# The product with w_out of a hybrid encoder block, as seven products of sums of quarters

## The chip, the cores and the metric

One Trainium2 chip, one of its cores. The program is one launch that computes the whole block. Five engines run side by side, each with its own instruction stream: TensorE (PE, matmuls and transposes), VectorE (DVE), ScalarE (ACT), GpSimd (POOL) and SyncE (SP, which here only issues transfers). Transfers move between DRAM and the on-chip memory (SBUF) on 16 DMA engines. Matmuls write into banks of PSUM, from which DVE or ACT read them ("evict"). The metric is the device time of one launch in microseconds (us).

## The reference

x is 1024 tokens by 1024 features, float32; 16 meta tokens are put ahead and dropped at the end.

```python
u = rmsnorm(h, norm_mix)
a, q, k, v, r, lr, ga, gb = split(u @ w_in)
p = multiscale_pool(a) through w_pool_mix, times pool_scale
y_a = p @ w_pool_out
log_a = log_sigmoid(lr @ w_gate_up + b_gate) / 16
o = gla_chunked(q * 64 ** -0.5, k, v, log_a)        # chunks of 64 tokens
o = rmsnorm(o, gla_norm) * silu(r)
y_b = o @ w_gla_out
m = sigmoid(ga) * y_a + sigmoid(gb) * y_b
h = h + m @ w_out                                    # 1024 x 1024 by 1024 x 1024
h = h + square(relu(rmsnorm(h, norm_ffn) @ w_ff1)) @ w_ff2
out = rmsnorm(h, norm_final)
```

The change is about the line `h + m @ w_out` and what stands beside it.

## The kernel before

Every product runs on PE in a float32 of two parts: an operand a is split into `hi` (rounded by an ACT copy) and `lo = a - hi` (a DVE subtract), and `mm3` (L275 and on) issues three matmuls per block of 128 of the contraction: hi x hi, hi x lo, lo x hi. So each weight or token that enters a product costs one ACT copy and one DVE subtract of its size.

The stages, in order of time: norm and transposes of x; the projections with w_in (with weights and tokens added and subtracted in quarters, so that four products become fewer); pooling; decays; the chunked attention, in two halves of 512 tokens (half 0 first), between whose steps blocks of `y_a` and `y_b` are poured; the merge stage; the first and second feed-forward layer (FF1, FF2), each by seven products of sums of quarters.

The merge stage, where the change lies, spans about 447 to 588 us:

- `yb_block(j, h)`: columns 256 j to 256 j + 255 of y_b for half h, two tiles of 128 columns (e = 0, 1), four k each. DVE evicts with the gate (L1195), adds y_a's part (L1196), ACT makes the hi (L1199) and DVE the lo (L1200) of m, in `MH[h]`, `ML[h]`. The gates and y_a's parts come back from DRAM (`gb_dram`, `ma_dram`) on SP's queue, by `ask` and `take`. Weights of w_gla_out come through the ring `W1` (two slots) and its raw buffers: load on SP, ACT copy at L84, DVE subtract at L85, tile names `raw`, `w1h`, `w1l`.
- `load_wo(ch, kk)`: a quarter of a column half of w_out, loaded on SP, split at L1344 (ACT) and L1345 (DVE) into `wo`.
- `out_tile(t, ch)`: the product for 128 tokens and 512 columns: eight k, 24 matmuls into a bank `mm` of which there are three; DVE adds it at L1379 onto `acc`, into which `x_again` had loaded x on SP. Behind the second column half comes `layer_norm` (ACT square L251, two small ACT operations, three small ones on DVE, the scaled row L259) and a store to `h_dram`.
- `turn_tile(t)`: eight PE transposes of a normed tile into banks `ms`, with ACT copies and splits for FF1, woven in two tiles behind the product.

PE's order is the order in which the code is written (`manual_schedule`); on the other engines the scheduler of the Tile layer puts instructions in an order at build time, by priorities that follow the order of the code, and each engine then runs its list strictly in order. A waiting instruction holds up all behind it on its engine. In the kernel before, POOL has 58 rows: sums of w_in's weights (L810) and a few others; all transfers of the stage are issued by SP.

Of the kernel before, what the change touches and what calls it, by code (L numbers as in the profile page):

```python
# [96 lines left out]
class Raw:  # L97
# [11 lines left out]
    def load(self, ap, n):  # L109
        while any(self.slots[self.n % len(self.slots)] is t for t in self.held):  # L110
            self.n += 1
        self.last = self.slots[self.n % len(self.slots)]
        dst = self.last[:, :n]
        self.n += 1
        view = dst
        if len(ap.shape) == 3:
            view = dst.rearrange("p (a b) -> p a b", a=ap.shape[1])
        self.nc.sync.dma_start(view, ap)
        return dst
# [3 lines left out]
def kernel(  # L123
# [55 lines left out]
    h_dram = dp.tile([8, P, D], F32, name="h_dram")  # L179
    hf_dram = [dp.tile([NPAIR, P, HALF], F32, name=f"hf{m}_dram") for m in range(7)]  # L180
# [425 lines left out]
    def decays(p):  # L606
        def fn():
# [6 lines left out]
            if p:  # L614
                act.activation(gnorm, gnorm, ACT.Copy, scale=0.5)
# [75 lines left out]

    def differences():
# [394 lines left out]
    def gla_open():  # L1087
        left.pop_to(S["left_t"])
        right.pop_to(0)
        S["yg"] = {h: right.push(f"yg{h}", [P, 2, HEADS, HALF], F32R) for h in (1, 0)}  # L1090
# [9 lines left out]
        wanted[:] = [("a", d, h) for d in range(8) for h in range(2)] + [("b", d, 0) for d in range(8)]  # L1100
# [68 lines left out]
    KEPT = (2, 3)  # L1169
    kept = {}  # L1170

    def yb_block(j, h):
        def fn(wb=None):
# [7 lines left out]
            yg = S["yg"][h]  # L1181
            for e in range(2):
                d, w = 2 * j + e, slice(e * P, (e + 1) * P)
                ask()
                gl, ml = take("b", d, h)
# [11 lines left out]
                th = MH[h][:, d]  # L1197
                tl = ML[h][:, d]
                act.activation(th, gl, ACT.Copy, scale=0.5)  # L1199
                dve.scalar_tensor_tensor(tl, gl, 0.5, f32(th), ALU.mult, ALU.subtract)  # L1200
# [132 lines left out]

    def load_wo(ch, kk):
        def fn():
            wo = S["wo"][ch][:, :, 2 * kk : 2 * kk + 2]
            c = slice(ch * HALF, (ch + 1) * HALF)
            src = w_out[kk * 256 : (kk + 1) * 256, c].rearrange("(k p) c -> p k c", p=P)
            if ch:
                r = raw.load(src, D).rearrange("p (k c) -> p k c", k=2)  # L1340
            else:
                r = S["acc"][:, 4 + kk].rearrange("p (k c) -> p k c", k=2)
                nc.sync.dma_start(r, src)
            act.activation(wo[:, 0], r, ACT.Copy)  # L1344
# [4 lines left out]
    step(rest, merge_open)
    def wo1_open():  # L1350
        raw.back()
        left.pop_to(S["left2"])
        right.pop_to(0)
        S["u2p"] = right.push("u2p", [P, 2, HALF], F32)
        raw.lend(right.push("rawx0", [P, D], F32))
        S["right_ff"] = right.mark()
        S["wo"].append(right.push("wo1", [P, 2, KT, HALF], F32R))


    ORDER = (0, 4, 1, 5, 2, 3, 6, 7)  # L1360

    def out_tile(t, ch):
        def fn():
            half, at = t // 4, (t % 4) * P
            wo = S["wo"][ch]
            if ch == 0 and t < 6:
                x_again(t + 2)
            if ch == 0 and t == 6:
                act.activation(gB, gB, ACT.Copy, scale=-0.5)
            b, n = bank("mm"), ORDER.index(t)  # L1370
            for j in range(2):
                if ch and j and n > 1:
                    turn_tile(ORDER[n - 2])
                mm3(
                    b, KT // 2, lambda i: (MH[half][:, 4 * j + i, at : at + P], ML[half][:, 4 * j + i, at : at + P]),
                    lambda i: (wo[:, 0, 4 * j + i], wo[:, 1, 4 * j + i]), first=j == 0, last=j == 1,
                )
            a = S["acc"][:, t, ch * HALF : (ch + 1) * HALF]
            dve.tensor_tensor(a, b, a, ALU.add)  # L1379
            if ch:  # L1380
                layer_norm(S["acc"][:, t], S["u2"][:, n % 2])
                nc.sync.dma_start(h_dram[t], S["acc"][:, t])

        return fn

    def turn_tile(t, tags=("ms",)):
# [3 lines left out]
        u, acc, g = S["u2"][:, ORDER.index(t) % 2], S["acc"], t % 4  # L1390
# [348 lines left out]
```

## Time and profile before

| what | value |
|---|---|
| time, median of 3 runs | 1210.76 us (1210.07 to 1211.37) |
| profiled execution, span from first to last instruction | 1209.1 us (its own time on the device is not listed; the median lies 1.7 us above the span) |
| mean granted PE clock | 0.998 |
| PE / DVE / ACT / POOL busy | 99% / 69% / 48% / 7% |
| bytes moved by DMA | 192.79 MB, mean 159 GB/s |

Times are read from one profiled execution. "Busy" is the time in which an engine executes an instruction; PE's instructions overlap, so a matmul of 0.39 us follows the one before by less. A group row reads: line, engine, operation, output<-input by names, shape, xcount | busy us, mean ns of one | idle time before them and who ended it. A row of the timeline reads: start, duration, engine, line, operation, and in brackets the idle time before it.

### The profile page before, as it was taken

Reading aid. Unit: us, or ns where it says so; the run is one execution under the profiler, and the core shown is the slowest. Engines: PE = TensorE matmul, PEld = TensorE weight load, DVE = VectorE, ACT = ScalarE, POOL = GpSimd, SP = SyncE. Lnnn points to the kernel's source line nnn. Section 1 sums busy time; section 2 is a strip of 40 time slices with the busy share of each in tenths; the row PEclk is TensorE's granted clock in tenths of the full one; section 3 lists DMA queues with packets and bytes.
Section 4 is the critical chain, followed back from the end, with each engine's and each line's share of the span. In section 5 each row is a group of like instructions: output and inputs, shape, how many; then the busy total and the mean of one; then the engine's idle time right before and its main releaser. Section 6 shows DMA issues by size and latency. Waiting matters only on the chain.

```text
span 1209.1 us, 18303 instructions
## 1 busy us (share of the span) xinstructions
PE 1194.4 (99%) x6775; PEld 993.1 (82%) x6775; DVE 837.5 (69%) x1369; ACT 574.4 (48%) x1014; POOL 79.1 (7%) x97
## 2 busy tenths in 40 slices
PE   9999999999999999999999999999999999999997
PEld 7999877878778887788788888888888888888886
DVE  6636567565686669726887767677675887887686
ACT  7546444444456124305655545455464444444554
POOL 0000062323320000000000000000000000000000
PEclk9999999999999999999999999999999999999999
DMA  8223253534348978812255444444479963333532
GB/s 245 77 60 123 91 133 110 166 110 146 112 138 296 315 218 268 284 32 87 88 161 168 151 139 157 148 160 151 152 253 318 348 229 98 98 100 91 173 96 88
DMA packets 151385, 192.79 MB, mean 159 GB/s; under 512 B 12216, under 2 KB 86256, under 8 KB 151296
## 3 DMA queue, kind: packets, MB, share of 16 engines
q1 hardware_dynamic: 151136, 191.56, 49.5%
q8 instruction: 53, 0.87, 0.3%
q14 instruction: 36, 0.29, 0.1%
q10 hardware_dynamic: 160, 0.07, 0.0%
HBM read 128.66 MB, written 62.93 MB: 158 GB/s over the span
## 4 chain that ended last, share of the span: by engine, by line
PE 68%; DVE 3%; issue 1%; DMA 1%; ACT 1%; DVEq 0%; ACTq 0%
PE b_oa L287 5%; PE b_oa L285 5%; PE b_oa L286 5%; PE b_y L285 4%; PE b_y L286 4%; PE b_y L287 4%; PE b_mm L285 4%; PE b_mm L287 4%; PE b_mm L286 4%; PE b_ob L287 4%; PE b_ob L285 4%; PE b_ob L286 4%; PE b_z L286 3%; PE b_z L285 3%; PE b_z L287 3%; PE b_sc L285 2%
## 5 line engine op out<-in xcount | busy, mean ns | idle before, releaser
L774 ACT ACTIVATE w1h<-raw 128x512 fp32r<-128x512 f32 x106 | 65.8, 622 | 51.2 <-PE b_sc L286 21.2
L285 PE MATMUL b_sc<-th,w1h 128*128 128x512 f32 x216 | 85.4, 395 | 0.4 <-ACT u2p L1522 0.4
L285 PE MATMUL b_z<-th,w1h 128*128 128x512 f32 x216 | 84.9, 393 | 0.4 <-DVE c L893 0.4
L775 DVE TENSOR_TENSOR w1l<-raw,w1h 128x512 fp32r<-128x512 f32 x106 | 72.5, 685 | 18.0 <-ACT w1h L774 18.0
L286 PE MATMUL b_sc<-tl,w1h 128*128 128x512 f32 x216 | 84.8, 393 | 0.0
L286 PE MATMUL b_z<-tl,w1h 128*128 128x512 f32 x216 | 84.2, 390 | 0.4 <-DVE tl L1408 0.4
L287 PE MATMUL b_sc<-th,w1l 128*128 128x512 f32 x216 | 84.4, 391 | 0.0
L287 PE MATMUL b_z<-th,w1l 128*128 128x512 f32 x216 | 84.1, 389 | 0.0
L774 ACT ACTIVATE w1h<-fs 128x512 fp32r<-128x512 f32 x81 | 51.1, 630 | 67.0 <-PE b_y L286 33.6
L775 DVE TENSOR_TENSOR w1l<-fs,w1h 128x512 fp32r<-128x512 f32 x81 | 57.7, 712 | 23.7 <-ACT w1h L774 23.7
L285 PE MATMUL b_mm<-th,w1h 128*128 128x512 f32 (+1 forms) x208 | 72.0, 346 | 0.0
L287 PE MATMUL b_mm<-th,w1l 128*128 128x512 f32 (+1 forms) x208 | 71.1, 342 | 0.0
L286 PE MATMUL b_mm<-tl,w1h 128*128 128x512 f32 (+1 forms) x208 | 71.0, 342 | 0.0
L774 ACT ACTIVATE w1h<-bt 128x512 fp32r<-128x512 f32 x46 | 29.1, 632 | 70.8 <-issue 43.9
L1598 DVE TENSOR_TENSOR bt<-w,w 128x512 f32<-128x512 f32 x80 | 54.7, 683 | 2.7 <-DMA w<-in_w_ff_dram 2.7
L285 PE MATMUL b_mm<-wo,th 128*128 128x512 f32 x128 | 50.4, 394 | 0.9 <-PE b_mm L287 0.9
L287 PE MATMUL b_mm<-wo,tl 128*128 128x512 f32 x128 | 49.9, 390 | 0.0
L286 PE MATMUL b_mm<-wo,th 128*128 128x512 f32 x128 | 49.8, 389 | 0.0
L285 PE MATMUL b_y<-wo,w1h 128*128 128x512 f32 x128 | 49.8, 389 | 0.0
L286 PE MATMUL b_y<-wo,w1h 128*128 128x512 f32 x128 | 49.8, 389 | 0.0
L287 PE MATMUL b_y<-wo,w1l 128*128 128x512 f32 x128 | 49.8, 389 | 0.0
L775 DVE TENSOR_TENSOR w1l<-bt,w1h 128x512 fp32r<-128x512 f32 x46 | 31.8, 691 | 25.6 <-ACT w1h L774 25.6
(425 smaller groups left out, 3317.1 us busy)
## 6 DMA issues: line engine op xcount, KB each, us to landing
hf_dram<-h SPq DMA_DIRECT2D x112, 256.0 KB, 2.1
raw<-hf_dram SPq DMA_DIRECT2D x112, 256.0 KB, 2.6
w<-in_w_ff_dram SPq DMA_DIRECT2D x64, 256.0 KB, 4.8
raw<-in_w_in_dram SPq DMA_DIRECT2D x22, 512.0 KB, 4.7
raw<-in_w_ff_dram SPq DMA_DIRECT2D x16, 512.0 KB, 4.1
rawx<-in_w_ff_dram SPq DMA_DIRECT2D x16, 512.0 KB, 4.1
rawp<-in_w_in_dram SPq DMA_DIRECT2D x10, 512.0 KB, 4.2
xs<-in_x_dram SPq DMA_DIRECT2D x8, 512.0 KB, 4.8
```

The source lines that it names most:

```text
L285: pe.matmul(ps, ah, bh, start=first and i == 0, stop=False, skip_group_check=more)
L286: pe.matmul(ps, ah, bl, start=False, stop=False, skip_group_check=more)
L287: pe.matmul(ps, al, bh, start=False, stop=last and i == n - 1, skip_group_check=more)
L774: act.activation(hi, a, ACT.Copy)
L775: dve.tensor_tensor(lo, a, f32(hi), ALU.subtract)
L1598: dve.tensor_tensor(bt, w, S["w2"][q[3:]][:, i], ALU.add if q[2] == "+" else ALU.subtract)
```

## The change

m (tokens by features) and w_out are each taken as two by two quarters of 512 by 512, and the product is made of seven products P1 to P7 of 512 x 512 x 512, four token tiles and four k each, instead of eight.

- Four sums of w_out's quarters are made in DRAM at the program's start: for each, a copy and an accumulating transfer, on POOL's queue (`sums_of_w_out`). Two of them are built on each other: the fourth on the third, the third on the second.
- Sums of m's quarters are made where y_b is finished: `split_to` and subtracts on DVE, `in_two` (two 128x256 halves) on POOL. One quarter of half 0 is stored to `a21_dram` and loaded again by POOL.
- Weights (`bring`) and x (`x_quarter`: a direct load and an accumulating one for each column half) come on POOL's queue, as loads of 1 MB or 2 x 512 KB. The lo parts of some weights are made by POOL (`parts(p, pool)`).
- The banks are mm 2, x 2, ms 2 instead of mm 3, ms 3; P1's first two tiles use the two-bank tile `b_sc`.
- m is kept without the factor 0.5, which moves into other scales (gnorm 0.25, pscale 0.5). Half 1's tokens come first in `acc` and at the end (`tokens`). w_gla_out's columns are taken as j and j + 4, loaded by two transfers.

The core of the diff:

```diff
+    def sums_of_w_out():
+        u1, u2, u3, u4 = sums_dram
+        b11, b12, b21, b22 = (w_out_quarter(j) for j in range(4))
+        for to, first, second in ((u1, b11, b12), (u3, b22, b12), (u2, u3, b11), (u4, u2, b21)):
+            pool.dma_start(to, first)
+            pool.dma_start(to, second, accum_op=ALU.add)
+
+    def in_two(op, to, a, b):
+        for c in (slice(0, 256), slice(256, HALF)):
+            pool.tensor_tensor(to[:, c], a[:, c], b[:, c], op)
...
+    step(one, lambda: sums_of_w_out())
...
                 dve.scalar_tensor_tensor(gl, gl, 1.0, b, ALU.add, ALU.mult)
                 dve.tensor_tensor(gl, gl, ml, ALU.add)
-                th = MH[h][:, d]
-                tl = ML[h][:, d]
-                act.activation(th, gl, ACT.Copy, scale=0.5)
-                dve.scalar_tensor_tensor(tl, gl, 0.5, f32(th), ALU.mult, ALU.subtract)
+                m.append(gl)
+                if h:
+                    after_half1(j, e, gl)
+                elif e == 0:
+                    nc.sync.dma_start(a21_dram[j], gl)
+                else:
+                    split_to(quarter(1), j, gl)
+                    dve.tensor_tensor(gl, m[0], gl, ALU.subtract)
+                    split_to(quarter(2), j, gl)
...
+    def after_half1(k, e, m):
+        s2, s3 = S["acc"][:, 4 + k, :HALF], S["tmp"][:, k]
+        if e == 0:
+            split_to(quarter(3), k, m)
+            in_two(ALU.subtract, s3, m, s3)
+            dve.tensor_tensor(s2, s2, m, ALU.subtract)
+            split_to(far(1), k, s2)
+        else:
+            split_to(S["w"][1], k, m)
+            in_two(ALU.add, s2, m, s2)
...
-        banks(keep=2, ms=3)
+        banks(keep=1, mm=2, x=2, ms=2)
...
+    def parts(p, eng=dve):
+        hi, lo = weights_of(p)
+        for k, a in enumerate(landed.pop(p)):
+            act.activation(hi[:, k], a, ACT.Copy)
+            if eng is pool:
+                in_two(ALU.subtract, lo[:, k], a, f32(hi[:, k]))
             else:
+                dve.tensor_tensor(lo[:, k], a, f32(hi[:, k]), ALU.subtract)
...
+        mm3(b, 4, lambda k: (ah[:, k, c], al[:, k, c]), lambda k: (wh[:, k], wl[:, k]), first=first, more=not first)
+        if p == "P5":
+            act.activation(c22, b, ACT.Copy)
+            return
...
+    out_products("P5", 0, 1, 2, 3)
+    later(lambda: parts("P2"))
+    yb(0)
+    later(second_copy)
+    later(lambda: x_quarter(1, 1, True))
+    yb(1)
+    later(lambda: bring("P1", two_raws()))
+    later(lambda: x_quarter(0, 0))
+    later(lambda: x_quarter(0, 1, True))
+    later(third_parts)
+    later(lambda: bring("P6", [S["tmp"]]))
+    out_products("P2", 0)
+    later(lambda: parts("P1", pool))
+    out_products("P2", 1, 2, 3)
...
+    later(lambda: bring("P4", two_raws()))
+    later(lambda: parts("P7", pool))
+    later(lambda: parts("P4", pool))
+    later(early_blocks)
+    out_products("P6", 0, 1)
+    out_products("P3", 0)
+    out_products("P6", 2)
+    out_products("P3", 1)
+    out_products("P6", 3)
+    later(turn_tile, 0)
```

How the built order moves, at three places. First DVE where half 0's y_b is finished, before: from one split of w_gla_out's weights (L85) to the next; `sr` and `yg` belong to the attention's output, `o` and `c` are tiles of m.

```order
L85 TENSOR_TENSOR w1l<-raw_116,w1h 128x1024
L1269 TENSOR_TENSOR sr_3829<-b_m_4528,sr_3829 128x1024
L1196 TENSOR_TENSOR o<-o 128x512
L1195 SCALAR_TENSOR_TENSOR o<-o,b_mm 128x512
L1272 TENSOR_TENSOR yg_3805<-sr_3829,yg_3805 128x1024
L1200 SCALAR_TENSOR_TENSOR tl_136<-o,th_132 128x512
L1196 TENSOR_TENSOR o<-o,t_985 128x512
L1269 TENSOR_TENSOR sr_3833<-b_sc,sr_3833 128x1024
L1200 SCALAR_TENSOR_TENSOR tl_136<-o,th_132 128x512
L85 TENSOR_TENSOR w1l<-raw_120,w1h 128x1024
```

The same engine and place in the changed program, the last ten rows up to the second split (L1237 and L1238 are the evict and the add, L1210 the lo parts, L1246 the new subtract).

```order
L1238 TENSOR_TENSOR o<-o,t_990 128x512
L1237 SCALAR_TENSOR_TENSOR t_990<-t_990,b_mm 128x512
L1330 TENSOR_TENSOR fo<-sr_3843,fo 128x1024
L1210 TENSOR_TENSOR tl_141<-o,th_137 128x512
L1238 TENSOR_TENSOR t_990<-t_990 128x512
L1246 TENSOR_TENSOR o<-o 128x512
L1237 SCALAR_TENSOR_TENSOR c<-c,b_mm 128x512
L1210 TENSOR_TENSOR tl_149<-o,th_145 128x512
L1238 TENSOR_TENSOR c<-c 128x512
L85 TENSOR_TENSOR w1l<-raw_125,w1h 128x1024
```

Between the two splits stand 13 instructions now, ten of them 512 wide, where eight stood, five of them 512 wide.

Second POOL, in the changed program, behind half 1's last y_b block: L713 are its half operations, L1432 loads of weights, L1409 the direct load of an x quarter. In the program before, POOL has nothing at this place.

```order
L713 TENSOR_TENSOR tmp<-acc,tmp 128x256 x2
L713 TENSOR_TENSOR wo_4714<-raw_121,wo_4714 128x256 x2
L713 TENSOR_TENSOR wo_4714<-raw_125,wo_4714 128x256 x4
L1432 DMA raw_121<-in_w_out_dram 128x2x512
L713 TENSOR_TENSOR acc<-acc 128x256 x2
L1432 DMA raw_125<-in_w_out_dram 128x2x512
L1409 DMA acc<-in_x_dram 128x4x512
L1432 DMA tmp<-sum_dram 128x4x512
```

The load of x for the first column half, which SP issued before, stands behind eight half operations and two loads of weights.

Third ACT ahead of the first norm, before: splits of w_out (L1344) and of the first w_ff1 block (L774), then the square of the norm (L251).

```order
L1344 ACTIVATE wo_4933<-raw_120 128x1024
L774 ACTIVATE w1h<-raw_116 128x512 x2
L1344 ACTIVATE wo_4933<-rawx_4929 128x1024
L774 ACTIVATE w1h<-rawx_4929 128x512 x2
L251 ACTIVATE u_4679,small<-acc 128x1024
```

In the changed program (L1439 are the hi parts of w_out's sums, L798 those of w_ff1, L258 the square):

```order
L1439 ACTIVATE th_145<-raw_121 128x512 x2
L1439 ACTIVATE th_145<-raw_125 128x512 x2
L1439 ACTIVATE wo_4714<-tmp 128x512 x4
L1439 ACTIVATE th_145<-raw_121 128x512 x2
L1439 ACTIVATE th_145<-raw_125 128x512 x2
L798 ACTIVATE w1h<-raw_121 128x512 x2
L798 ACTIVATE w1h<-raw_125 128x512 x2
L258 ACTIVATE u_4704,small<-acc 128x1024
```

The square comes behind four w_ff1 splits as before, but these now use the raw buffers in which the sums for P4 stood last, and so come behind the splits of P7's and P4's weights. The two loads for them stand on SP.

More of the change, by code (lines that the diff above doesn't have):

```diff
@@ L179 @@
     h_dram = dp.tile([8, P, D], F32, name="h_dram")
+    sums_dram = [dp.tile([HALF, HALF], F32, name=f"sum{n}_dram") for n in range(4)]
+    a21_dram = dp.tile([4, P, HALF], F32, name="a21_dram")
     hf_dram = [dp.tile([NPAIR, P, HALF], F32, name=f"hf{m}_dram") for m in range(7)]
@@ L1167, in rows4, with two_columns, far, quarter @@
         return w[:, j * 256 : (j + 1) * 256].rearrange("(k p) c -> p k c", p=P)
-    KEPT = (2, 3)
+    def two_columns(j):
+        return w_gla_out.rearrange("(k p) (u r c) -> p k u r c", p=P, u=2, c=P)[:, :, :, j]
+    KEPT, YA = (2, 3), (0, 2, 1, 3)
     kept = {}
+    def far(n):
+        return tuple(S["fo"][:, k, 4 * n : 4 * n + 4] for k in range(2))
+    def quarter(n):
+        half, k = n // 2, slice(4 * (n % 2), 4 * (n % 2) + 4)
+        return MH[half][:, k], ML[half][:, k]
+    def split_to(hl, k, a):
+        h, l = (x[:, k] for x in hl)
+        act.activation(h, a, ACT.Copy)
+        dve.tensor_tensor(l, a, f32(h), ALU.subtract)
     def yb_block(j, h):
@@ L1349 @@
[L1349 to L1384, printed above, removed]
@@ new lines, in merge_open, with tokens, x_quarter @@
+        bring("P2", [S["acc"][:, :4, HALF:]])
+        for k in MERGE:
+            h, l = (a[:, k] for a in quarter(2))
+            in_two(ALU.add, S["acc"][:, 4 + k, :HALF], f32(h), f32(l))
+        parts("P5")
+        nc.sync.dma_start(gB, bcast(norm_ffn))
+        act.activation(gB, gB, ACT.Copy, scale=-0.5)
+    step(rest, merge_open)
+    def tokens(a):
+        t = (a + 4) % 8
+        return slice(t * P, (t + 1) * P)
+    def x_quarter(r, c, add=False):
+        to = S["acc"][:, 4 * r : 4 * r + 4, c * HALF : (c + 1) * HALF]
+        src = x[(1 - r) * HALF : (2 - r) * HALF, c * HALF : (c + 1) * HALF].rearrange("(t p) c -> p t c", p=P)
+        if add:
+            pool.dma_start(to, src, accum_op=ALU.add)
+        else:
+            pool.dma_start(to, src)
@@ L1410, in turn_tile @@
         dve.tensor_tensor(lo, b[1], t1, ALU.subtract)
         dve.tensor_tensor(b12, b[1], b12, ALU.subtract)
-        dve.tensor_tensor(hi, hi, lo, ALU.subtract)
-        for n, a in enumerate((lo, b12)):
-            fh, fl = (S["wo"][0][:, k, 4 * n : 4 * n + 4, cols] for k in range(2))
-            act.activation(fh, a, ACT.Copy)
-            dve.tensor_tensor(fl, a, f32(fh), ALU.subtract)
-    def yb(j):
-        step(rest, yb_block(j, 1), *(() if j in KEPT else (W1, [rows4(w_gla_out, j)])))
@@ L1437, in load_ff, with far_split, later, out_products @@
+    def far_split(n, cols, a):
+        fh, fl = (x[:, :, cols] for x in quarter(n))
+        act.activation(fh, a, ACT.Copy)
+        dve.tensor_tensor(fl, a, f32(fh), ALU.subtract)
+    def yb(j):
+        step(rest, yb_block(j, 1), *(() if j in KEPT else (W1, [two_columns(j)])))
+    def later(fn, *args):
+        step(rest, lambda: fn(*args))
+    def out_products(p, *tiles):
+        for t in tiles:
+            later(product, p, t)
     def load_ff(i, u):
         load_block(w_ff1, i, u, 2 * i * P)
-    def first_blocks():
+    def early_blocks():
```

194 lines of the change are left out of this document (127 added, 67 removed).

## The prediction

> **What bounds the kernel now.** I read the page first, then the table of windows, then the waits of PE alone. Line numbers in rows are those of the kernel before; rows of the changed program have numbers of its own.
>
> ```profile
> span 1209.1 us, 18303 instructions
> PE 1194.4 (99%) x6775; PEld 993.1 (82%) x6775; DVE 837.5 (69%) x1369; ACT 574.4 (48%) x1014; POOL 79.1 (7%) x97
> L285 PE MATMUL b_mm<-wo,th 128*128 128x512 f32 x128 | 50.4, 394 | 0.9 <-PE b_mm L287 0.9
> L287 PE MATMUL b_mm<-wo,tl 128*128 128x512 f32 x128 | 49.9, 390 | 0.0
> L286 PE MATMUL b_mm<-wo,th 128*128 128x512 f32 x128 | 49.8, 389 | 0.0
> ```
>
> PE is busy 99% of the span: any matmul less shortens the run, and any new wait of PE lengthens it. The product with w_out is 3 x 128 = 384 matmuls. The windows (us; PE, PEld, DVE, ACT and POOL busy with their counts, then clock, DMA share, GB/s) show what room the other engines have:
>
> ```profile
> 5.00:10.00 5.00, 5.00 (x22) 3.62 (x22) 2.45 (x6) 3.81 (x9) 0.00 (x0) 1.00 1.04 364
> 20.00:25.00 5.00, 5.00 (x44) 4.96 (x43) 4.66 (x9) 4.91 (x12) 0.00 (x0) 1.00 0.90 288
> 450.00:480.00 30.00, 29.75 (x138) 24.11 (x137) 28.52 (x39) 12.62 (x16) 0.00 (x0) 1.00 0.76 246
> 480.00:510.00 30.00, 28.33 (x124) 23.18 (x125) 21.01 (x31) 10.00 (x13) 0.00 (x0) 1.00 0.90 305
> 510.00:540.00 30.00, 30.00 (x134) 24.86 (x133) 9.36 (x13) 3.37 (x5) 0.00 (x0) 1.00 0.18 54
> 540.00:570.00 30.00, 30.00 (x146) 25.07 (x145) 16.16 (x33) 13.37 (x29) 0.00 (x0) 1.00 0.17 70
> ```
>
> Three things count: in 450 to 480, where half 0's y_b is finished, DVE is 95% busy; in 480 to 510 the transfers are; behind 510 the old product left DVE, ACT and the transfers nearly empty. In the opening the transfers are full. What PE waits for from 440 to 612 (total, times, longest):
>
> ```profile
> PE b_mm L285 <- DVE o L1195: 0.9, 1, 0.9
> PE b_mm L285 <- PE b_mm L287: 0.9, 1, 0.9
> PE b_sc L285 <- ACT u2p L1522: 0.4, 2, 0.3
> PE b_z L286 <- DVE tl L1408: 0.4, 1, 0.4
> PE b_mm L287 <- DVE w1l L85: 0.2, 1, 0.2
> ```
>
> So 2.8 us in all, of which the first two and the last, 2.0, lie in the stage that is rewritten.
>
> **What the change removes.** Seven products of four tiles, four k and three matmuls are 336, so 48 go. Back to back they follow each other so (first and last of 27 rows of the timeline of PE: 26 steps in 5.89 us, 0.2265 each):
>
> ```profile
> 519.70 0.39 PE L286 MATMUL b_mm<-wo,th 128*128 128x512 f32 x1
> 525.59 0.39 PE L285 MATMUL b_mm<-wo,th 128*128 128x512 f32 x1
> ```
>
> 48 x 0.2265 = **10.9 us less**, and a block of 12 is 2.72 us. Nothing else can be gained, but for the 2.0 us of old waits: the transposes and both layers behind are the same work. The question is what PE waits for instead. I walked through the built order by these durations.
>
> **1. Half 0's y_b, DVE first.** Subtracts and stores for the sums of tokens stand ahead of the low half of the next w_gla_out weights. The stretch before:
>
> ```profile
> 457.63 1.22 DVE L85 TENSOR_TENSOR w1l<-raw,w1h 128x1024 fp32r<-128x1024 f32 x1
> 463.45 1.22 DVE L1269 TENSOR_TENSOR sr<-b_sc,sr 128x1024 f32<-128x1024 f32 x1
> 464.58 0.68 DVE L1200 SCALAR_TENSOR_TENSOR tl<-o,th 128x512 fp32r<-128x512 f32 x1
> 465.18 1.23 DVE L85 TENSOR_TENSOR w1l<-raw,w1h 128x1024 fp32r<-128x1024 f32 x1
> 466.46 0.50 PE L287 MATMUL b_mm<-yg,w1l 128*128 128x512 f32 x1 [0.15 <-DVE w1l L85]
> ```
>
> A 512-wide instruction takes a slot of 0.60 (464.58 to 465.18), a 1024-wide one 1.14 (463.45 to 464.58). Between the two splits stood 3 wide and 5 narrow; now 3 wide and 10 narrow, 3.0 us more, and the first split itself is later by a wide and a narrow one less an idle stretch that fills, about 1.6. The second split is 4.6 late, and PE had no slack (it waited 0.15). **4.6 us** (3.0 if only the five narrow ones count, 5.0 at most).
>
> **2 to 5. Loads, banks and tokens of P5 and P2.** These hang on ACT, POOL and transfers:
>
> ```profile
> L1199 ACT ACTIVATE th<-o 128x512 fp32r<-128x512 f32 x7 | 4.4, 625 | 10.9 <-DVE o L1196 10.9
> L810 POOL TENSOR_TENSOR s<-rawp,rawp 128x256 f32<-128x256 f32 x10 | 7.2, 739 | 15.3 <-DVE w1l L775 15.3
> L810 POOL TENSOR_TENSOR fs<-raw,fs 128x256 f32<-128x256 f32 x12 | 11.7, 994 | 20.3 <-DVE w1l L775 17.4 <-DVE small L1045 2.9
> 152.92 1.43 POOL L810 TENSOR_TENSOR s<-raw,raw 128x256 f32<-128x256 f32 x2
> 189.74 2.40 POOL L810 TENSOR_TENSOR fs<-raw,fs 128x256 f32<-128x256 f32 x2 [1.21 <-DVE w1l L775]
> raw<-hf_dram SPq DMA_DIRECT2D x112, 256.0 KB, 2.6
> raw<-in_w_ff_dram SPq DMA_DIRECT2D x16, 512.0 KB, 4.1
> raw<-in_w_gla_out_dram SPq DMA_DIRECT2D x6, 512.0 KB, 4.8
> acc<-in_x_dram SPq DMA_DIRECT2D x8, 512.0 KB, 6.9
> gi<-gi_dram SPq DMA_DIRECT2D x4, 768.0 KB, 7.9
> 466.44 0.38 SPq L118 DMA_DIRECT2D raw<-in_w_gla_out_dram  x1
> ```
>
> POOL issues no load in the trace, nor does any row move 1 MB or accumulate. For the new 1 MB loads I take 6 us to land, between the 512 KB rows of 4.1 and 6.9, since the transfers thin out behind 510; the ends are 2.6 and 7.9 with 0.4 to 1 for the issue. A POOL half subtract (128x256) I take at 0.8, ends 0.72 (half of 1.43) and 1.2 (half of 2.40).
>
> (2) P5's sums can be loaded only when DVE has done the last subtract of half 0, some 479.4, and land at 486.5 with a split of 0.63 + 0.68 behind; PE arrives at 486.9. **1.0** (0 to 3.3). (3) Only two mm banks are left, and P5's first tile is copied out by ACT behind splits that wait for POOL's token sums and DVE's adds: **2.5** (0 to 3.3). (4) P2's second k needs the last y_b tile of half 1, through evict, add, ACT and split: 0.6 + 0.6 + 0.63 + 0.68 + the issue gaps, about 3.2 behind its product, while PE has 0.7 of work (k 0): 2.3 to 3.5, the upper end if ACT's split waits for POOL's sum of that tile; **3.0**. (5) P2's sums are added onto the x quarter of the first column half. Its load stands on POOL behind six half subtracts, a w_out load, two more half subtracts and another load, and waits for the last token split too: issued some 4 us behind the last y_b product, landed at 10, added at 10.7. P2's third tile, which needs the first one's bank, is ready at 3.2 + 2.0 + 2.7 = 7.9; with the issue gaps and POOL's two loads counted both ways **4.0** (0.8 with a landing of 2.6, 6.7 with 7.9).
>
> The page "DMA: Bandwidth & Descriptors" of the Trainium skill, section "Anatomy of one DMA — SWDGE (gpsimd) path", fits a GpSimd-issued transfer as 2.0 us plus bytes over 436e3 per us, 4.4 for 1 MB; by it, an estimate, term 5 would be 2.4 and the forecast 1.6 lower, while the rows above have 512 KB at up to 6.9 in this stage, and I keep to the rows.
>
> (6) Product P1's first two tiles, P6's and P7's lie in one two-bank tile b_sc, and PE's second waits for DVE to read the first: an evict of 0.68 and its start, 1.45 where it queues behind two others, then 0.85 and 0.85: **3.1** (0 to 3.2).
>
> **7. The first transpose.** It needs the norm of tile 0, whose chain runs as here, from the evict to the scaled row, 4.2 us (550.27 to 554.47) and 3.5 of it from ACT's square:
>
> ```profile
> 545.55 1.06 ACT L251 ACTIVATE u<-acc 128x1024 f32<-128x1024 f32 x1 [24.60 <-DVE acc L1379]
> 550.27 0.69 DVE L1379 TENSOR_TENSOR acc<-b_mm,acc 128x512 f32<-128x512 f32 x1 [1.23 <-PE b_mm L287]
> 550.99 1.06 ACT L251 ACTIVATE u<-acc 128x1024 f32<-128x1024 f32 x1 [3.73 <-DVE acc L1379]
> 553.19 1.28 DVE L259 SCALAR_TENSOR_TENSOR u<-acc,small,gB 128x1024 f32<-128x1024 f32 x1
> ```
>
> Before, ACT had been idle for 24.6 us at the first square; now it stands behind four splits of w_ff1, whose two loads wait for POOL to finish P7's and P4's 16 half subtracts, which begin when P1's last tile is done (call that T). With 0.8 each POOL ends at T+11.5; the second load lands 4.4 later and its two splits end at T+17.5, the square and its chain at T+21. PE has six blocks, 16.3, and 0.85 of wait from (6): it is there at T+17. **4.2** with the next transposes (1.5 with 0.72 and 4.1; 7.5 with 1.0 and 4.8).
>
> **8. The opening.** Eight 1 MB steps run DRAM to DRAM from POOL's queue, two at once, then one behind the other, from about 3 us; the transfers there are at 0.9 to 1.04 of their share and feed the first products. Bounds: nothing, since other transfers of that time end ahead of need, up to 5 (one 512 KB row of 4.8 late). I take **2.0**. POOL waits at each step, so its mask cast and this MEMSET stand behind five serial steps:
>
> ```profile
> 70.23 0.98 POOL L626 MEMSET lr<- 96x1056 f32 x1 [43.09 <-PE b_mm L287]
> 75.54 0.17 ACT L410 ACTIVATE lr<-b_ms 16x16 fp32r<-16x16 f32 x1
> ```
>
> At twice 4.8 each the steps end at 51, ahead of 70; they would have to take 14 us each to be late for 75.
>
> **The sum**, against the span of 1209.1 (the median of the runs shown, 1210.76, is 1.7 more): -10.9 - 2.0 + (4.6 + 1.0 + 2.5 + 3.0 + 4.0 + 3.1 + 4.2 = 22.4) + 2.0 = +11.5, so 1220.6, and **1222** as a run. All low ends together (3.0 + 0 + 0 + 2.3 + 0.8 + 0 + 1.5 = 7.6, opening 0) give -5.3, 1205; all high ends (5.0 + 3.3 + 3.3 + 3.5 + 6.7 + 3.2 + 7.5 = 32.5, opening 5) give +24.6, 1235.
>
> **Rivals.** *POOL is never last (not slower).* Terms 2, 3, 5 and 7 all have POOL in their chain. If it runs its list at 0.72 a half subtract, issues in 0.4 and its loads land in 2.6 to 4.1, these four fall away and 4 goes to 2.3: -12.9 + 4.6 + 2.3 + 3.1 + 2.0 = -0.9, 1210, and down to 1205 without the waits of 6 and the opening. For it: transfers at 0.18 of their share behind 510. Against it: in the built order POOL gets 56 half operations and 18 transfers in this stage, and its program order puts x behind them. It decides where terms 2, 3, 5 and 7 sum to under 0.9, which needs the x load issued within 3 us of the last y_b product.
>
> *POOL and DVE block each other.* The 994 ns against 739, and 2.40 against 1.43 for a pair, show POOL slower where DVE is at work. At 1.2 a half subtract, term 7 grows by 16 x 0.4 = 6.4 and the others little: 1228. The page "SBUF — State Buffer" of the Trainium skill (section "Terms", "shared port pair") has the two engines hold one pair of ports in turn, exclusively, the loser blocked for a whole instruction; the rows of POOL show a third to two thirds more time beside DVE, which agrees with a block now and then.
>
> *The sums hold up POOL's MEMSET.* If a step takes over 14 us, ACT's copy at 75.5 and all decays behind it wait: each us over is five; 16 us a step are +10 on the rest: 1232 or more.
>
> **How the numbers follow.** My forecast, with its bounds, 0.64; POOL never last 0.22 (1205 to 1213; it holds faster 0.13 and the same 0.09); POOL and DVE blocking 0.09; the MEMSET 0.05. A difference of 0.2%, 2.4 us, is about what a measurement of this kernel can tell from none: faster 0.14, same 0.10, slower 0.76, the hundredths beside the rival's from the low end of my own bounds. The range 1205 to 1235 holds forecast, blocking and the not slower rival down to its end.
>
> **What would show it.** In the profile after: PE's matmul count down by 48 and its busy time by some 11; waits of PE near 470 on w1l (4.6), at P5 on ACT's copies, at P2's third tile on the add of x's load, at the first transpose on the norm. ACT's square behind the w_ff1 splits and these behind their loads would prove 7. I am wrong if PE's waits from 440 to 590 stay under 13 us, or if the opening's windows lose more than 5 us of PE.

## The result, and the profile after

The changed kernel takes 1277.57 us (median of 4 runs, 1275.3 to 1280.04) beside 1211.07 for the kernel before on the same chip (1210.07 to 1213.17): ratio 1.0553, 95% interval 1.0534 to 1.0571, so 66 us slower. 1222 was forecast, at most 1235. The page of the profile after (span; busy times with counts; the clock in 40 slices):

```profile
span 1275.9 us, 18427 instructions
PE 1206.4 (95%) x6727; PEld 995.8 (78%) x6727; DVE 861.7 (68%) x1397; ACT 591.4 (46%) x1055; POOL 159.0 (12%) x187
PEclk9899999999999999979999999999998999999999
```

PE has the 48 matmuls less, yet is busy 12.0 us longer (1206.4 against 1194.4). Without them it should have lost 10.9, so 22.9 us of its busy time are new, and the third row says where most of them come from: the clock falls. The mean granted clock is 0.978, before 0.998. The rest is idle time: span less busy is 69.5 us, before 14.7, so +54.8; and 54.8 + 12.0 = 66.8 is the whole difference of the spans. Where it lies is told by the windows, after (columns as in the prediction; the last lies where FF2 starts):

```profile
0.00:30.00 30.00, 21.12 (x102) 14.88 (x102) 12.77 (x25) 13.28 (x27) 4.62 (x11) 1.00 1.01 278
30.00:60.00 30.00, 23.70 (x178) 23.70 (x179) 14.96 (x28) 18.89 (x43) 2.29 (x4) 0.83 0.90 259
440.00:700.00 260.00, 222.84 (x1105) 177.25 (x1104) 179.56 (x283) 108.08 (x198) 74.45 (x82) 0.94 0.51 159
930.00:960.00 30.00, 22.84 (x101) 18.58 (x99) 19.12 (x30) 14.42 (x24) 0.00 (x0) 0.94 0.54 177
```

and the same view of the kernel before, for the opening and for the merge stage with the start of FF1:

```profile
0.00:30.00 30.00, 28.10 (x170) 22.80 (x171) 20.71 (x41) 23.53 (x52) 2.37 (x8) 1.00 0.83 245
30.00:60.00 30.00, 29.98 (x248) 29.57 (x247) 20.37 (x33) 18.13 (x40) 0.00 (x0) 1.00 0.26 79
440.00:700.00 260.00, 257.25 (x1239) 211.77 (x1236) 184.71 (x295) 116.12 (x200) 0.00 (x0) 1.00 0.47 157
```

Each row's length less PE's busy time is its idle time: in the opening 15.2 us against 1.9, from 440 to 700 37.2 against 2.8, at the start of FF2 7.2. The transfers of the opening, at 0.26 of their share from 30 to 60 before, are at 0.90 now. The third place is the start of FF2. Its wait and the opening's longest, from the waits of PE (total, times, longest); what ACT waits for during the opening's; and two rows of the transfers issued up to 70 us (KB each, median us to landing), then one of the same view before:

```profile
PE b_sc L526 <- ACT xr L532: 9.8, 1, 9.8
PE b_oa L292 <- ACT w1h L798: 7.3, 1, 7.3
34.02 1.06 ACT L554 ACTIVATE vw<-raw 128x1024 fp32r<-128x1024 f32 x1 [10.15 <-DMA raw<-in_w_in_dram]
...
raw<-in_w_in_dram SPq DMA_DIRECT2D x6, 512.0 KB, 13.4
sum_dram<-in_w_out_dram POOLq DMA_DIRECT2D x6, 1024.0 KB, 12.8
...
raw<-in_w_in_dram SPq DMA_DIRECT2D x7, 512.0 KB, 5.2
```

The 512 KB loads of w_in, which feed the first products, take 13.4 us instead of 5.2. ACT waits 10.15 us for one of them, and the copy of xr that PE waits for stands behind that on ACT. The waits of PE from 430 to 700, after:

```profile
PE b_mm L292 <- ACT wo L1209: 6.1, 1, 6.1
PE b_ms L1498 <- DVE u L266: 5.5, 2, 3.7
PE b_mm L292 <- DVE acc L1467: 4.9, 1, 4.9
PE b_mm L292 <- ACT w1h L84: 3.0, 1, 3.0
PE b_sc L292 <- ACT u2p L1666: 3.0, 1, 3.0
PE b_sc L292 <- DVE acc L1467: 2.5, 1, 2.5
PE b_mm L292 <- DVE acc L1237: 2.1, 1, 2.1
PE b_mm L292 <- ACT wo L1439: 1.7, 1, 1.7
PE b_sc L292 <- DVE acc L1465: 1.6, 2, 0.8
PE b_mm L294 <- DVE w1l L85: 1.3, 2, 0.8
PE b_mm L292 <- ACT acc L1461: 1.2, 1, 1.2
```

But for the one on u2p, which lies in FF1, these are the waits that the prediction named, most of them longer. What follows one of them, in the timeline of PE (start, duration, and in brackets the wait; the 2.5 of the sixth row):

```profile
569.45 0.50 PE L292 MATMUL b_sc<-wo,th 128*128 128x512 f32 x1 [2.49 <-DVE acc L1467]
...
571.27 0.63 PE L292 MATMUL b_sc<-wo,th 128*128 128x512 f32 x1
571.70 0.63 PE L293 MATMUL b_sc<-wo,th 128*128 128x512 f32 x1
...
574.36 0.39 PE L294 MATMUL b_x<-wo,tl 128*128 128x512 f32 x1
574.59 0.39 PE L292 MATMUL b_x<-wo,th 128*128 128x512 f32 x1
```

A us behind the wait the same matmul takes 0.63 instead of 0.39 and follows its neighbour by 0.43 instead of 0.23, for 3.4 us. Then the clock is back. The longest stretches of this kind are 10.2 us; one stands at the wait of 6.1 us in the merge stage, the other two at the two waits shown of the opening and of FF2 (windows of after):

```profile
31.40:41.60 10.20, 5.30 (x25) 5.30 (x26) 5.26 (x11) 7.49 (x17) 1.12 (x2) 0.51 0.92 326
956.40:966.60 10.20, 6.47 (x15) 4.80 (x16) 3.44 (x6) 2.89 (x5) 0.00 (x0) 0.51 0.97 336
```

With the 0.94 from 440 to 700 (31 us at half) the stretches sum to some 51 us. PE is idle in 4.9 and 3.7 of the two rows and in about 5 of the 31, so it works for 37 us at 0.2265 / 0.43 of its pace, which costs 37 x 0.47 = 17. The other 5 or 6 of the 22.9 fit the ends of bursts, an estimate: the last matmul ahead of each wait shows its whole 0.39 where it otherwise shows 0.23, with some 30 waits. In the kernel before there is no such stretch ahead of the last 5 us.

### The profile page after: what moved, and what is told of

The parts are those of the page before. It is cut to its first block, busy times and chain, and to the rows that moved or that the text cites. A ratio compares the mean times of both kernels' runs of the same rounds, so it can differ in the third digit from the quotient of the medians.

```text
span 1275.9 us, 18427 instructions
## 1 busy us (share of the span) xinstructions
PE 1206.4 (95%) x6727; PEld 995.8 (78%) x6727; DVE 861.7 (68%) x1397; ACT 591.4 (46%) x1055; POOL 159.0 (12%) x187
## 5 line engine op out<-in xcount | busy, mean ns | idle before, releaser
L798 ACT ACTIVATE w1h<-raw 128x512 fp32r<-128x512 f32 x114 | 70.8, 623 | 83.0 <-PE b_sc L293 35.8
L799 DVE TENSOR_TENSOR w1l<-raw,w1h 128x512 fp32r<-128x512 f32 x114 | 78.0, 685 | 34.4 <-ACT w1h L798 34.3
L798 ACT ACTIVATE w1h<-fs 128x512 fp32r<-128x512 f32 x81 | 50.9, 630 | 62.3 <-PE b_y L293 32.0
L798 ACT ACTIVATE w1h<-bt 128x512 fp32r<-128x512 f32 x46 | 29.1, 632 | 70.6 <-issue 45.2
L292 PE MATMUL b_sc<-fo,w1h 128*128 128x512 f32 x128 | 50.7, 396 | 3.0 <-ACT u2p L1666 3.0
L294 PE MATMUL b_y<-th,w1l 128*128 128x512 f32 x128 | 49.9, 390 | 0.9 <-DVE w1l L799 0.9
L294 PE MATMUL b_sc<-fo,w1l 128*128 128x512 f32 x128 | 50.3, 393 | 0.0
L292 PE MATMUL b_y<-th,w1h 128*128 128x512 f32 x128 | 49.9, 390 | 0.4 <-ACT w1h L798 0.4
L293 PE MATMUL b_sc<-fo,w1h 128*128 128x512 f32 x128 | 50.3, 393 | 0.0
L293 PE MATMUL b_y<-tl,w1h 128*128 128x512 f32 x128 | 49.8, 389 | 0.0
L292 PE MATMUL b_oa<-w1h 128*128 128x512 f32 x104 | 41.6, 400 | 7.3 <-ACT w1h L798 7.3
L292 PEld LDWEIGHTS b_z<-th,w1h 128*128 128x128 f32 x216 | 40.5, 188 | 9.6 <-DVE c L917 0.8
L1643 ACT ACTIVATE h<-h 128x512 f32<-128x512 f32 x48 | 30.3, 632 | 37.5 <-DVE h L1683 25.1
```

The lines of the kernel that those rows point to most:

```text
L292: pe.matmul(ps, ah, bh, start=first and i == 0, stop=False, skip_group_check=more)
L293: pe.matmul(ps, ah, bl, start=False, stop=False, skip_group_check=more)
L294: pe.matmul(ps, al, bh, start=False, stop=last and i == n - 1, skip_group_check=more)
L798: act.activation(hi, a, ACT.Copy)
L799: dve.tensor_tensor(lo, a, f32(hi), ALU.subtract)
L1643: act.activation(h, h if b is None else b, ACT.Relu)
```

## The experiments

After the result the theory was that three things besides the forecast waits make the time: the accumulating transfers crowd the opening; FF2's first weights wait for memory that FF1's tokens now hold to the end; and each wait of PE of some length is followed by half the clock. Its rivals: that the waits in the merge stage are all POOL's doing, its order of issue above all, and that the clock is a by-product which costs nothing of its own. All ratios are against the kernel before on the same chip. A difference between two changed kernels is one of medians, in part from different chips, on which the kernel before itself lies between 1209.5 and 1211.1; so it is good to 1 or 2 us.

**The sums at a later time.** `e1_sums_later` has the sums of w_out behind the decays' MEMSET on POOL, from 71 us on; the same transfers, nothing else.

```diff
-            pool.dma_start(to, first)
+            tc.keep_in_program_order(pool.dma_start(to, first))
             pool.dma_start(to, second, accum_op=ALU.add)
...
-    step(one, lambda: sums_of_w_out())
     for f, i in ((a_, 0), (d_, 0), (a_, 1), (d_, 1), (m_, 0), (a_, 2), (m_, 1), (a_, 3), (m_, 2), (k_, 0), (m_, 3)):
         f(i)
+    step(one, lambda: sums_of_w_out())
```

> The changed kernel with the sums of w_out's quarters issued behind POOL's MEMSET of lr (87 us in the profile of the changed kernel), ahead of the weight sums, where the transfers are at a quarter of their share. Theory: the eight 1 MB steps in the opening delay the loads of w_in (13.4 us to land where 4.7 was usual), PE idles 9.8 us at one place and 13 us in all, and the clock is halved for 10.2 us behind it; all of it goes, so the profile has at most 3 us of idle PE before 60 us, no halved clock there, and the time falls by 16 to 18, from 1277.6 to about 1261. Rival: the opening is late because POOL's mask cast and MEMSET stand behind the steps or for another reason than the transfers; then PE's 9.8 us wait for the copy of xr stays and the time falls by less than 5.

Measured: 1261.67 us, ratio 1.0431 (1.0415 to 1.0446), 15.9 us less than the changed kernel (14.4 where each is taken against the kernel before on its own chip). The windows of the opening, and one of POOL's issues in this kernel's timeline (start, duration; in brackets POOL's wait):

```profile
0.00:30.00 30.00, 28.04 (x170) 22.78 (x171) 20.75 (x40) 23.42 (x53) 2.42 (x8) 1.00 0.83 245
30.00:60.00 30.00, 29.98 (x248) 29.57 (x247) 20.35 (x34) 18.12 (x40) 0.00 (x0) 1.00 0.26 79
...
91.43 1.01 POOL L709 DMA_DIRECT2D sum_dram<-in_w_out_dram  x1 [11.19 <-DMA sum_dram<-in_w_out_dram]
```

The opening is the kernel before again to 0.1 us. The accumulating steps still take 10 to 11 us, and POOL waits up to 11.2 for one, but nothing near hangs on it: PE is busy for 367.6 us from 60 to 430, before for 367.7. The same 8 MB cost 14 to 16 us at 3 us after the start and nothing that shows at 71. The cast and the MEMSET on POOL are not the reason: they ran at 60 and 87 us, behind the opening's wait. The opening's share of the loss is thus shown, of which 13.3 are idle time.

**FF2's first weights in another place.** In `e2_ff2_place` the quarter of w_ff2 that is loaded first lies where FF1's tokens of P1 and P2 lay, which are done with earlier.

```diff
-        S["w2"] = {q: left.push("w2_" + q, [P, NPAIR, HALF], F32) for q in ("11", "21", "22", "12")}
+        S["w2"] = {q: left.push("w2_" + q, [P, NPAIR, HALF], F32) for q in ("21", "22", "12")}
         S["c"] = left.push("c", [P, 8, D], F32)
+        S["w2"]["11"] = right.push("w2_11", [P, NPAIR, HALF], F32)
```

> The changed kernel with the first quarter of w_ff2 in the place on the chip that the products P1 and P2 of the first layer leave, instead of that of P5 and P3. Theory: the wait of 7.3 us at the start of the second layer is a wait for a place: the first load can only start when the last product of the first layer has read its tokens; with the other place it starts four blocks (10.9 us) sooner, the wait goes below 1 us and the halved clock of 10.2 us behind it goes too, so the time falls by about 11 (7.3 plus 3 to 5 of clock), to about 1267. Rival: the transfers are too slow there anyway; then the wait shrinks by 2 us at most.

Measured: 1271.91 us, ratio 1.0512 (1.0496 to 1.0528). The waits of PE from 920 to 1000 hold one row, where the changed kernel has 7.3:

```profile
PE b_oa L293 <- DVE fxl L799: 0.3, 1, 0.3
```

The wait is gone, so its cause was the place. The half clock behind it is gone too (1.00 from 930 to 990). The time fell by 5.7 (4.1 against the kernel before on each chip), half of what was expected: from 430 to 700 PE idles for 39.1 us in this run, in the changed kernel for 37.2. On top of e1 the same edit (`e5_both`, below) is worth 9.2.

**A wait by itself.** To price a wait without any other part of the change, `e3_holds_before` puts 10, 14 and 20 ACT copies (128x512, 0.63 us each) into the kernel before, ahead of three tiles of the old product, on which PE then waits; `e12_holds_filled` gives PE 22, 20 and 37 matmuls to do in the same holds, which nobody reads.

```diff
             b, n = bank("mm"), ORDER.index(t)
+            if ch == 0:
+                for _ in range({3: 10, 5: 14, 7: 20}.get(t, 0)):
+                    act.activation(wo[:, 0, 0], f32(wo[:, 0, 0]), ACT.Copy)
+                fill = {3: 22, 5: 20, 7: 37}.get(t, 0)          # e12 alone
+                if fill:
+                    f = bank("ms")
+                    for _ in range(fill):
+                        pe.matmul(f, MH[half][:, 1, at : at + P], wo[:, 0, 1], start=True, stop=True)
```

> The kernel before with three holds of PE of different length in the product with w_out, where all else is idle: 10, 14 and 20 ACT copies of a block of weights onto itself ahead of tiles 3, 5 and 7 of the first column half (the result is the same). By 0.55 to 0.63 us a copy and 4.8 us of work that covers them, PE idles about 1, 3.5 and 7 us. Theory that an idle PE gets a halved clock: behind the first nothing, behind the second 3.4 us at half clock, behind the third 10.2 us, so the time rises by the 11.5 us of idle and 4 to 6 more, to about 1227. Rival, that a wait costs its own length: the granted clock stays 1.0, the time rises by 11.5, to about 1222.

> e3 with its three holds of PE (5.2, 4.6 and 8.6 us of idle) filled with matmuls that nobody reads: 22, 20 and 37, together 17.9 us at 0.2266 each. The chain of copies and all else stays. Theory of the halved clock: the idle time goes, the clock stays at 1.0 through the product, and the time rises over the kernel before by the length of the holds alone, 17.5 to 19, where e3 rose by 26.0. Rival, that the 7.6 us of e3 beyond its idle time come from the copies on ACT holding up other work: the time stays at +25 to +27.

Measured: holds 1235.56 us, ratio 1.0213 (1.0196 to 1.023), +26.0; filled 1229.05, 1.0162 (1.0145 to 1.0179), +19.5. From e3 the wait's row, a piece of PE's timeline, and a window:

```profile
PE b_mm L285 <- ACT wo L1373: 18.4, 3, 8.6
516.95 0.80 PE L285 MATMUL b_mm<-wo,th 128*128 128x512 f32 x1 [5.16 <-ACT wo L1373]
...
522.24 0.63 PE L285 MATMUL b_mm<-wo,th 128*128 128x512 f32 x1
523.04 0.40 PE L287 MATMUL b_mm<-wo,tl 128*128 128x512 f32 x1
515.00:525.00 10.00, 8.05 (x23) 6.39 (x24) 1.95 (x3) 2.98 (x5) 0.00 (x0) 0.66 0.18 52
```

and from e12 the same window, where all that is left of the row of waits is 0.3 us:

```profile
515.00:525.00 10.00, 10.00 (x46) 8.29 (x45) 1.99 (x3) 4.40 (x8) 0.00 (x0) 1.00 0.17 49
```

Three waits, 18.4 us in all, cost 26.0. With PE at work through the same holds they cost 19.5, about their length, and the clock stays at 1.00. So the halved clock is a price of its own, 6.5 us here (the difference of two kernels on two chips), 0.35 us for each us waited; in the changed kernel 17 for 54.8 is 0.31, or 0.42 with the ends of bursts. That the clock costs nothing falls.

The page "TensorE: Matmul & The Clock Gate" of the Trainium skill, section "What's actually happening", has a free-running window of 3413 ns: after one idle window the array runs at half clock, after one busy window at full. The stretches of 3.4, 6.8 (behind each of the three holds) and 10.2 us are multiples of that window, which agrees; the wait of 2.49 us above is shorter than it and was followed by 3.4 us of half clock all the same, so as a threshold for one wait the page's figure is too high for this trace.

**Who issues the loads.** `e4_loads_by_sp` gives the new loads of the stage to SP, so that they no longer stand behind POOL's subtracts.

```diff
-            pool.dma_start(S["tmp"][:, k], a21_dram[k])
+            nc.sync.dma_start(S["tmp"][:, k], a21_dram[k])
...
-            pool.dma_start(to, src)
+            nc.sync.dma_start(to, src)
...
-            pool.dma_start(a, src[:, k : k + n])
+            nc.sync.dma_start(a, src[:, k : k + n])
```

> The changed kernel with the loads of the product with w_out (sums, quarters, the stored quarter of y_b, the two direct x quarters) issued by SP; only the accumulating transfers stay on POOL. Theory that POOL's order sets the waits of P2's third tile, P1 and the first transpose: the wait of 4.9 us for the add of x falls under 2, and the time falls by 4 to 10. Rival, that the transfers themselves and the chain of y_b's last tile set them: the waits of 6.1 and 4.9 stay within 1 us and the time within 3.

Measured: 1274.63 us, ratio 1.0536 (1.052 to 1.0552), whose interval overlaps that of the changed kernel. The waits ahead of P2's second k and of its third tile, 6.1 and 4.9, are 6.2 and 5.8 here, so POOL's order of issue is not what sets them. P5's wait for its weights went from 1.7 to 5.9, so for that load SP's queue was no better a place.

**Both cures, and PE kept busy.** `e5_both` is e1 and e2 together. `e6_warm` adds 68 matmuls that nobody reads, ahead of P5 (10), of P2's first (22) and third tile (18) and of the first transposes (18).

```diff
+    def warm(n):
+        h = quarter(1)[0]
+        b = bank("ms")
+        for i in range(n):
+            pe.matmul(b, h[:, 0, :P], h[:, 0], start=True, stop=True)
...
+    later(warm, 10)
     out_products("P5", 0, 1, 2, 3)
...
+    later(warm, 22)
     out_products("P2", 0)
...
+    later(warm, 18)
     later(turn_tile, 0)
```

> The edits of e1 and e2 together, as the base of the next three. If the two costs are independent, the savings of 15.9 and 5.7 add up to a time of about 1256, or down to 1251 if the halved clock behind the second layer's start goes in full; the wait for the copy of xr and the one at the start of the second layer are both under 1 us, and what is left over the kernel before lies between 480 and 660 us.

> e5 with matmuls on PE whose result nobody reads, placed where PE waits in the product with w_out: 10 ahead of P5 (2.3 us), 22 ahead of P2's first tile (5.0), 18 ahead of P2's third tile (4.1), 18 ahead of the first transpose (4.1), 15.4 us of work in all. Theory of the halved clock: the waits shrink by what fills them (each stays below 2 us), the clock stays at 1.0 from 500 to 610 us, and the time falls by 6 to 10 against e5 although work was added. Rival, that the waits cost their length and the clock is a by-product: the time stays within 2 of e5 or rises.

Measured: e5 1252.45 us, ratio 1.035 (1.033 to 1.037), 25.1 less than the changed kernel (24.3 against the kernel before on each chip). e6 1253.1, 1.035 (1.0333 to 1.0366): no gain, though no loss either from 68 x 0.2265 = 15.4 us of added work. The filled waits shrank (6.1 to 1.2, 4.4 to 2.7), but this row, 0.7 in e5, came up in e6; below it ACT's timeline, one row of e5 and two of e6:

```profile
PE b_mm L292 <- ACT acc L1461: 6.7, 1, 6.7
...
497.32 0.60 ACT L1461 ACTIVATE acc<-b_mm 128x512 f32<-128x512 f32 x1
...
501.84 0.63 ACT L1209 ACTIVATE th<-tmp 128x512 fp32r<-128x512 f32 x1 [3.57 <-POOL tmp L713]
...
502.89 0.58 ACT L1461 ACTIVATE acc<-b_mm 128x512 f32<-128x512 f32 x1
```

It is the copy of P5's first tile on ACT. In e5 it stands ahead of a split that waits for POOL's token sums (that split ran at 501.02), in e6 behind it: with the new matmuls the built order on ACT moved as well. So there is a new wait, and from 500 to 530 the clock is 0.84. The expectation was missed, and e6 does not tell whether filled waits pay in this stage, since it changed two things. PE starts P2's second k 4.1 us later than in e5, with 7.2 us of work added ahead of it.

**Another order.** `e7_p1_first` is e5 with P1, whose tokens are there earlier, ahead of P2.

```diff
-    later(lambda: parts("P2"))
+    later(lambda: parts("P1"))
...
-    out_products("P2", 0)
-    later(lambda: parts("P1", pool))
-    out_products("P2", 1, 2, 3)
+    out_products("P1", 0)
+    later(lambda: parts("P2", pool))
+    out_products("P1", 1, 2, 3)
+    out_products("P2", 0, 1, 2, 3)
...
```

> e5 with product P1 ahead of P2 (their weights change places, P6 runs through ahead of P3). P1 needs half 1's first y_b tiles only and its four tiles lie in four banks. Theory that P2's two waits come from what it needs too soon, the last y_b tile's tokens (6.2) and the load of x behind that tile (5.3): both go and the time falls by 11 to 20 against e5, their length and one or two halved clocks. Rival, that transfers and DVE are simply full in this stage: the same waits turn up at P1 or P6 and the time moves by less than 5.

Measured: 1254.19 us, ratio 1.0363 (1.0342 to 1.0385), no gain. Two rows, four waits in all, take the place of the longest ones of e5:

```profile
PE b_sc L292 <- DVE acc L1467: 16.1, 3, 11.3
PE b_ms L1498 <- DVE small L262: 13.7, 1, 13.7
```

**Single links of the chain.** Four kernels on top of e5. `e8_ln_pin` puts the first splits of w_ff1 behind the second transposed tile. On e8, `e9_no_pool_math` makes the token sums and POOL's weight splits on DVE, `e10_no_x_load` drops the load of x under P2, so that a quarter of the output lacks x, and `e11_neither` does both.

```diff
-    later(lambda: ff_weights())                             # e8
...
     later(turn_tile, 1)
+    later(lambda: ff_weights())
...
-        for c in (slice(0, 256), slice(256, HALF)):         # e9
-            pool.tensor_tensor(to[:, c], a[:, c], b[:, c], op)
+        dve.tensor_tensor(to, a, b, op)
...
-    later(lambda: x_quarter(0, 0))                          # e10
...
-        if p == "P5":
-            act.activation(c22, b, ACT.Copy)
+        if p in ("P5", "P2"):
+            act.activation(c22 if p == "P5" else c11, b, ACT.Copy)
```

> e5 with the splits of the first w_ff1 blocks held behind the second transposed tile in ACT's and DVE's order. Theory: the first transpose waits (7.0 with the next) for a norm whose square stands behind these splits, and these for loads that wait for POOL; the wait falls below 2.5 us and the time by 4 to 9. Rival, that the norm comes late because its product's eviction is late: the wait stays above 5 us.

> e8 with all of POOL's half operations in the product with w_out (56 of 128x256, 0.73 to 1.29 us each) made by DVE as 28 of 128x512 (0.68); POOL only issues transfers. Theory that POOL's pace, with DVE and POOL slowing each other, is in the chain of P5's copies, P2's tokens, the norms: these waits (3.5 and 0.7, 6.2, 3.7 and 1.8) lose half or more, the wait for x (5.9) some 2, and the time falls by 7 to 14 from 1249.6. Rival, that DVE becomes the bound (28 x 0.6 = 17 us more in a stage of 110): the time stays within 3 or rises.

> e8 without the load of the x quarter onto which P2 is added; P2 is copied out by ACT instead, so that quarter of the output lacks x. Theory: the load of 1 MB, issued behind two others, costs the wait of 5.9 and its halved clock: P2's third tile waits under 1 us and the time falls by 6 to 9. Rival, that what is won there is lost again at P1's tiles or at P6's weights, which come over the same queue: the waits for b_sc (3.7 and 2.4) grow and the time falls by under 3.

> Both edits of e9 and e10 on e8 (the same quarter of the output lacks x). If the waits are independent, the gains add up, to about 1230; if one chain runs through all of them, the sum falls short by the larger part of the smaller gain.

| kernel | us | ratio (95%) | sum of PE's waits, 430 to 700 |
|---|---|---|---|
| e5 | 1252.45 | 1.035 (1.033 to 1.037) | 38.8 |
| e8 | 1249.61 | 1.0325 (1.031 to 1.0341) | 36.3 |
| e9 | 1246.75 | 1.0295 (1.0275 to 1.0316) | 34.4 |
| e10 | 1243.74 | 1.0273 (1.0255 to 1.0292) | 30.3 |
| e11 | 1242.53 | 1.0263 (1.0248 to 1.0279) | 30.6 |

One wait row of e8 (P2's third tile on the x load), then two rows of PE's timeline in e9, at P5 and at P2's second k:

```profile
PE b_mm L292 <- DVE acc L1469: 5.9, 1, 5.9
498.32 0.76 PE L292 MATMUL b_mm<-wo,th 128*128 128x512 f32 x1 [6.92 <-ACT wo L1210]
...
527.37 0.80 PE L292 MATMUL b_mm<-th,wo 128*128 128x512 f32 x1 [3.55 <-ACT wo L1210]
```

In e8 the waits of the transposes on the norm fall from 6.9 to 1.8 in all, as the step on ACT's order said, while others grow: 2.8 us, within the intervals and less than the 4 to 9 expected. In e10 the wait of 5.9 is gone, and the sum of waits falls by 6.0 and the time by 5.9 (5.5 against the kernel before on each chip): this link is shown. In e9 P2's second k waits 3.5 instead of 6.2 and P2's third tile 3.5 instead of 5.9, so POOL's arithmetic is in both chains. But P5, which waited 3.5 for its weights in e8, now waits 6.9 for a split of tokens on ACT. The edit also gives DVE 28 instructions more, and which of the two makes the new wait is not shown. e11 gains 7.1 where e9 and e10 gain 2.9 and 5.9. Some 30 us of waits stay in all of them.

No kernel here beats the kernel before. The best one with a whole output is e9, 3% slower.

## Why the prediction was wrong

The side was right, and so were most of the places. The size was not: +66.8 in the span where +11.5 stood. The gap of 55 us has four parts: PE's longer busy time, most of it the clock, 22.9, merge and FF1 waits 14.0 (34.4 + 2.0 - 22.4), opening 11.3 (13.3 - 2.0), FF2 7.3. One sign of being wrong that the prediction gave came true, an opening that loses more than 5 us of PE.

**The step that failed most** is the price of a wait: from "any new wait of PE lengthens it" on, each wait went into the sum at its length alone. The prediction's rows all had the clock at 1.00, since no wait of PE in the stage before is over 0.9 us, and so showed nothing of it. e3 and e12 show that a wait of some length is paid a second time; by e3's 0.35 the forecast's own 24 us of waits would have cost some 8 more, an estimate.

**Term 8** had bounds of 0 to 5 and cost 14 to 16 (e1), 13.3 of it idle. It took its steps at 9.6 us by doubling a quiet 512 KB row; the accumulating ones took 10.5 to 16.4. The larger error was to look at when the steps end instead of at what they do to the loads beside them, 5.2 to 13.4 us, in windows that stood at 0.9 to 1.04 of their share and were quoted as such.

**"Both layers behind are the same work"** is true of the work and false of the memory under it. FF1's tokens had changed places, and the 7.3 us at FF2's start came of that (e2). FF1's first transposes and products also waited some 4 us against 0.8 before, in no term.

**The merge terms**, forecast and then measured in PE's waits: (1) split of w_gla_out 4.6, 4.3; (2) P5's load 1.0, 2.5; (3) P5's banks 2.5, 3.3; (4) P2's second k 3.0, 6.5; (5) x under P2 4.0, 4.9; (6) b_sc 3.1, 4.1; (7) transposes 4.2, 6.5. Together 22.4, 32.1. That (1) came out is partly luck: at the split near 470 it meant, PE waited 0.5; the rest came at the next block, where ACT's half of the split stands behind a token split that waits 2.6 for DVE's new subtract. The longest miss is (4). Three rows of after lie between the evict of the last y_b tile, which ran on DVE from 538.01 to 538.69, and ACT's split of it at 542.95:

```profile
537.45 2.43 POOL L713 TENSOR_TENSOR tmp<-acc,tmp 128x256 f32<-128x256 f32 x2 [0.63 <-DVE acc L1238]
541.09 0.70 DVE L1210 TENSOR_TENSOR fo<-acc,fo 128x512 fp32r<-128x512 f32 x1 [1.80 <-ACT fo L1209]
541.71 1.21 DVE L1238 TENSOR_TENSOR acc<-acc 128x512 f32<-128x512 f32 x1
```

The prediction let the add (541.71) follow the evict at once. On DVE it stands behind a split of the tile before; that split waits for ACT, and ACT for POOL's token sum, two halves of 1.2. So the add begins 3.0 us after the evict ends, and takes 1.21 instead of 0.6 beside POOL. The rival that *POOL and DVE block each other* was partly true in that, and the Trainium skill's page "SBUF — State Buffer" (section "Terms"), cited there, agrees in kind. What POOL's arithmetic is worth in all is not known: e9 gains 2.9 us with the same work moved to DVE. For (5), the x load was issued at 548.6 and landed 7.5 us later; 6 was taken. The 4.4 weighed there, by the Trainium skill's page "DMA: Bandwidth & Descriptors" (section "Anatomy of one DMA — SWDGE (gpsimd) path"), was further off.

**The rivals.** *POOL is never last* falls: every term with POOL in its chain was there. *The sums hold up POOL's MEMSET* falls too. MEMSET came late, but it waited for PE, whose opening was late; from POOL's timeline after:

```profile
86.92 0.98 POOL L634 MEMSET lr<- 96x1056 f32 x1 [25.62 <-PE b_mm L294]
```

**Left open.** How the remaining 30 us of waits from 430 to 700 divide between DVE, ACT, POOL and the transfers. Most single cures moved part of their wait to another place (e6, e7 and e9 most plainly), and no run names one link that would bring the stage below the old one. A version with the sums kept on chip was not tried.

## What to carry to other kernels

Where PE runs at 99%, price its waits by their length and a third to two fifths more, once some 2 us of them fall close together; here seven products for eight save 10.9 us, and three such waits of 3 us undo it. Transfers between DRAM and DRAM are not free at a time when the loads that feed the first products fill the transfer engines: the same ones half a stage later cost nothing that shows. Where tiles change places, look at what later stages lay on the memory that is freed, and who reads it last.

## What the runs showed of the hardware that was not expected

The clock changes on a fixed grid. In windows of 0.02 us the half clock of after begins at 31.24, 488.62, 509.10, 539.82, 556.88, 570.54, 601.26, 652.46 and 956.24, and each lies a whole number of steps of 3.413 us behind the first. In these traces what decides is how long PE idles within one such step, not the length of one wait. Two steps of after:

```profile
485.21:488.63 3.42, 1.53 (x6) 0.97 (x6) 3.29 (x6) 1.68 (x3) 0.00 (x0) 1.00 0.95 307
488.63:492.04 3.41, 3.41 (x10) 2.63 (x9) 1.35 (x3) 0.63 (x1) 0.54 (x1) 0.50 1.11 371
```

PE idles 1.9 us in the first, in parts of two waits (3.0 and 0.8), and works through the second at half clock. From 440 to 1230 us in after and in e1, e2 and e4 to e9, a step at full clock with up to 1.6 us idle was never followed by half clock, one with 2.0 or more always; in between both occur. So the half clock of after begins 2.3 to 5.3 us after PE stops, according to where the wait lies on the grid, and a wait that is over can still slow the products behind it: that of 2.49 us ended at 569.45, and the half clock begins at 570.54.

An issue of SP itself took longer in the crowded opening; from the timeline of SP's queue after:

```profile
15.29 5.19 SPq L516 DMA_DIRECT2D xm<-in_meta_tokens_dram  x1
```

5.19 us for an issue that took 0.42 in the profile before; the two of w_in behind it took 4.92 together, before 2.98. No run tests this by itself.
